# A two-layer prefix DiT block on one core: the opening of layer 0 rearranged by quarters of scale and shift

## The chip, the cores and the metric

The kernel runs on one core of a Trainium2 chip. A core has TensorE (PE, with its weight loads shown as PEld), VectorE (DVE), ScalarE (ACT), GpSimd (POOL) and SyncE (SP), which here only issues transfers. The metric is the device time of one execution in microseconds: the median of three runs is 1883.46 us, from 1881.46 to 1883.66.

## The reference, cut to what matters

256 tokens of 2048 features and 256 context tokens go through two layers. The change touches layer 0, the Fourier branch, for both streams:

```python
shift, scale, gate = split(silu(c) @ ada_w[i] + ada_b[i], 3)
h = _rmsnorm(x, norm_g[i]) * (1 + scale) + shift
def _fourier_branch(h, w_in, w_mix):          # D_BRANCH = 4096
    u, z = split(h @ w_in, 2)                 # u: 16 groups of 256
    f = fft2(ug, axes=(1, 3), norm='ortho').real
    f = einsum('bngc,gcd->bngd', f, w_mix)
    return f * silu(z)
x = x + gate * (y @ w_out[i])
```

The context stream does the same with its own scale, shift and gate from c_ctx. Layer 1 is windowed attention with a sink, and a final norm follows; neither is touched.

## The kernel before, in words

All products are made of three passes: each fp32 operand is split into a high part h, rounded to a faster matrix type on ACT, and a rest l, on DVE (split, L60 and L61), and mm3 (L73 to L75) adds wh·xh, wh·xl and wl·xh in PSUM. The features of the model lie on the partitions in 16 blocks k of 128; both streams stand side by side in 512 columns. The layer has five stages.

- The opening (L148 to L322). The tokens xn come in four tiles of 128 rows, their squares are summed on ACT (L162) and the root taken (L81 to L85). In each of four steps of 512 features, the tokens are scaled by r and split (xh, xl: L212, L213), and a DFT over the tokens is made on PE, 12 passes per k, into PSUM. PE also works on the scale and the shift: `ada_pe` (L180) multiplies 32 pieces of ada_w of 1 MB, in_awp, by the conditioning; `ada_fin` turns a row of 512 results to the partitions (L184, L187, L188). `evac_hx` (L193 to L198) scales the transformed tokens with 1 + scale as it takes them out of PSUM into hx. The shift touches only column 0 of the transform (f0, L310 to L314). While the 16 pieces of shift come in, parts of groups 0 and 1 and the special columns run in between (u_step, sp_step), placed by a list of positions.
- The middle stage (from L329): 16 groups, each with a part "m" and a part "p" of 48 passes, weights wu loaded as sums and differences (load_uh, L122 on POOL and L123 on DVE), a small combined matrix (load_m) and a `mix` of 14 passes that writes two of 32 blocks of 128 features to DRAM (fd).
- The gate stage: 32 blocks z, 48 passes of 512 columns each. Its input hs is made anew from x transposed in DRAM (xT), with r, scale and shift (make_hs, L446 to L448). The first four blocks accumulate side by side over k; the other 28 come one by one. z_out (L455, L456) applies silu and multiplies the block that came back from fd. From block 4 on, each block also takes one job of the row sums for the other scales (ada_jobs, L418, on DVE).
- The output product of layer 0 (32 steps), with the rest of those jobs.
- Layer 1.

The order on each engine is chosen by a scheduler from the written order and its own estimate of times; `issue_after` adds an order by hand. Large weights pass through `raw`, three buffers of 1 MB, on SP's queue; in the opening raw_st adds two more (raw2), so that five are in turn. `ws` has six buffers of half splits, `act` 34 tiles of 128x512, PSUM eight banks. hx fills 32 of the 34 act tiles.

Of the kernel before, what the change touches and what calls it, by code (L numbers as in the profile page):

```python
# [10 lines left out]
F32 = mybir.dt.float32  # L11
# [12 lines left out]
GD = 256  # L24
EPS = 1e-6
# [3 lines left out]
def tile_dit(ctx: ExitStack, tc: tile.TileContext, a: dict, out: bass.AP):  # L29
# [113 lines left out]
    hx = []  # L143
    us = ctx.enter_context(ExitStack())
    sta = ctx.enter_context(ExitStack())
    sx = sta.enter_context(tc.tile_pool(name="sx", reuse_waits="tile", bufs=1))
    with tc.tile_pool(name="st", reuse_waits="tile", bufs=1, side="right") as st:
        xn = [sx.tile([P, D], F32, name=f"xn{t}") for t in range(4)]  # L148
        pre = {}
        pre[1, 0, 0] = raw(a["awp"][1, 0, 0])  # L150
        for t in range(4):
            nc.sync.dma_start(xn[t], a["x2"][t * P : (t + 1) * P, :])
        dump = st.tile([P, D], F32, tag="raw2", name="dump", bufs=2)
        dm = sx.tile([P, 2, N], F32, name="dm")
# [4 lines left out]
        ss = st.tile([P, 4], F32, name="ss")  # L159
        rr = st.tile([P, 4], F32, name="rr")  # L160
        for t in range(4):
            S.activation(dump, xn[t], AF.Square, accum_out=ss[:, t : t + 1])  # L162
            r1 = rsqrt(st, ss[:, t : t + 1], 1, f"r{t}")
            V.tensor_copy(rr[:, t : t + 1], r1)
# [3 lines left out]
        def raw_st(src):  # L168
            cnt[0] += 1
            if cnt[0] % 5 < 3:  # L170
                return raw(src)
            t = st.tile([P, D], F32, tag="raw2", name="raw2", bufs=2)
            nc.sync.dma_start(t[:, : src.shape[-1]], src)
            return t

        def ada_pe(o, which, nb, kgs):
            for kg in kgs:
                t = pre.pop((which, nb, kg)) if (which, nb, kg) in pre else raw_st(a["awp"][which, nb, kg])
                for j in range(4):
                    PE.matmul(o[j * 32 : (j + 1) * 32, :], c32[:, kg * 4 + j, :], t[:, j * 512 : (j + 1) * 512], start=kg == 0, stop=kg == 3)  # L180

        def ada_fin(o, dst, add):
            rows = st.tile([P, 512], F32, tag="rows", name="rows")
            S.copy(rows, o)  # L184
            o2 = psum()
            for j in range(4):
                PE.matmul(o2[:, j * 2 : (j + 1) * 2], rows[:, j * P : (j + 1) * P], sel, start=True, stop=True)  # L187
            V.tensor_tensor(dst, o2[:, 0:8].rearrange("p (a b) -> p a b", b=2), add, op=ALU.add)  # L188

        def evac_hx(nb, os_):  # L190
            for j in range(4):
                o, k = os_[j], nb * 4 + j
                V.tensor_tensor(f0[:, k, :], o[:, 0::N], gs0[:, k, :], op=ALU.mult)  # L193
                h, l = act(F32R), act(F32R)
                for s in range(2):
                    q = slice(s * N, (s + 1) * N)
                    S.activation(h[:, q], o[:, q], AF.Copy, scale=gs0[:, k, s : s + 1])
                    V.scalar_tensor_tensor(l[:, q], o[:, q], gs0[:, k, s : s + 1], h[:, q].bitcast(F32), op0=ALU.mult, op1=ALU.subtract)  # L198
                hx.append((h.rearrange("p (s j) -> p s j", s=2), l.rearrange("p (s j) -> p s j", s=2)))

        f0 = st.tile([P, KT, 2], F32, name="f0")
        prev = None
        for nb in range(4):
            oa = psum()
            ada_pe(oa, 1, nb, (0, 1))
            if prev is not None:
                evac_hx(nb - 1, prev)
            xh = sx.tile([P, 4, 512], F32R, tag="xh", name="xh")
            xl = sx.tile([P, 4, 512], F32R, tag="xl", name="xl")
            for t in range(4):  # L210
                xs = xn[t][:, nb * 512 : (nb + 1) * 512]
                V.tensor_scalar(xh[:, t], xs, rr[:, t : t + 1], None, op0=ALU.mult)  # L212
                V.scalar_tensor_tensor(xl[:, t], xs, rr[:, t : t + 1], xh[:, t].bitcast(F32), op0=ALU.mult, op1=ALU.subtract)  # L213
            prev = []
            for j in range(4):
                o = psum()
                for s in range(2):
                    for tt in range(2):
                        q = slice(j * P, (j + 1) * P)
                        mm3(o[:, s * N : (s + 1) * N], xh[:, s * 2 + tt, q], xl[:, s * 2 + tt, q], dh[:, tt, :], dl[:, tt, :], tt == 0, tt == 1)  # L220
                prev.append(o)
            ada_pe(oa, 1, nb, (2, 3))
            kq = slice(nb * 4, nb * 4 + 4)
            g4 = gs0[:, kq, :]
            ada_fin(oa, g4, adab[:, 0, 1, kq])
            V.scalar_tensor_tensor(g4, g4, 1.0, ng[:, 0, kq], op0=ALU.add, op1=ALU.mult)
# [53 lines left out]
        for nb in range(4):  # L280
            oa = psum()
            for kg in range(4):
# [6 lines left out]
                if pos == 2:  # L289
                    evac_hx(3, prev)  # L290
# [792 lines left out]
```

## Time and profile before

| what | value |
|---|---|
| median of 3 runs | 1883.46 us |
| span of the profiled execution | 1885.9 us (2.4 us above that median; no other time of it is given) |
| PE busy | 97% of the span |
| DVE, ACT, POOL busy | 75%, 50%, 13% |
| bytes moved by DMA | 359.61 MB, mean 191 GB/s |
| first 140 us | 47.63 MB, mean 340 GB/s |
| largest transfers of the opening | 32 pieces in_awp of 1 MB, 4 tiles of tokens, weights wu |

The page gives busy shares per engine and, in 40 slices of 47 us, the busy tenths, the granted TensorE clock and the DMA share. Matmuls are pipelined, so a busy PE isn't PE at its peak: the count of passes in a stretch tells its pace. A table by stretches shows busy time and count for each engine, then clock, DMA share and GB/s. A row of instructions has: line, engine, operation, output and inputs, count, busy time, mean in ns, and the idle time before it with what ended it.

### The profile page before, as it was taken

The page shows a single profiled execution, that of the slowest core. Times are in us where ns is not written, and L with a number is a line of the kernel's source. Part 1 is how long each engine was busy: PE and PEld are TensorE (multiplying, and loading weights), DVE is VectorE, ACT ScalarE, POOL GpSimd, SP SyncE. Part 2 cuts the span into 40 slices and gives each one's busy share as a digit, 9 for nine tenths or more (in the row PEclk, how much of TensorE's full clock was granted, in tenths as well). Part 3 has the DMA queues.
Part 4 walks back from the last instruction along what each step waited for, and adds up shares of the span by engine and source line. Part 5 has one row for each costly group of instructions (what it writes and reads, how often), then busy time and mean ns, then how long its engine had stood idle before and what let it go on. Part 6 is the DMA issues. An engine that isn't in the chain of part 4 may idle for free.

```text
span 1885.9 us, 26510 instructions
## 1 busy us (share of the span) xinstructions
PE 1832.5 (97%) x9921; PEld 1557.9 (83%) x9921; DVE 1412.7 (75%) x2743; ACT 941.1 (50%) x1634; POOL 239.3 (13%) x206
## 2 busy tenths in 40 slices
PE   6889999999999999999999999999999999999997
PEld 4569999888888888888888787888888888887886
DVE  5558999788777779687984744788788878887455
ACT  3334444442222233323322524788888888896443
POOL 0024344200000000000000001102211220200001
PEclk9899999999999999999999999999999999999999
DMA  9975555646656546764576323433333333434553
GB/s 384 381 258 181 196 195 180 233 173 253 243 207 255 213 190 228 285 223 158 199 263 264 112 96 128 138 131 124 123 134 124 123 120 130 176 134 162 196 179 134
DMA packets 60529, 359.61 MB, mean 191 GB/s; under 512 B 7601, under 2 KB 7745, under 8 KB 25329
## 3 DMA queue, kind: packets, MB, share of 16 engines
q1 hardware_dynamic: 49104, 324.83, 47.5%
q0 software_dynamic: 6720, 25.34, 3.6%
q10 hardware_dynamic: 4576, 7.74, 1.2%
q8 instruction: 78, 1.28, 0.3%
q14 instruction: 51, 0.41, 0.1%
HBM read 345.30 MB, written 12.59 MB: 190 GB/s over the span
## 4 chain that ended last, share of the span: by engine, by line
PE 88%; DVE 4%; DMA 3%; issue 3%; ACT 2%; POOL 1%; ACTq 0%; POOLq 0%; DVEq 0%; SPq 0%
PE ps L73 22%; PE ps L74 22%; PE ps L75 22%; PE ps L782 6%; PE ps L784 3%; PE ps L838 3%; PE ps L180 2%; PE ps L853 2%; PE ps L852 2%; PE ps L818 1%; PE ps L819 1%; DMA raw<-in_awp 1%; DVE wpl L61 1%; DMA raw<-in_wu 1%; POOL wm L122 0%
## 5 line engine op out<-in xcount | busy, mean ns | idle before, releaser
L60 ACT CAST wh<-raw 128x1024 fp32r<-128x1024 f32 x333 | 349.7, 1052 | 560.0 <-PE ps L74 485.7
L61 DVE TENSOR_TENSOR wl<-raw,wh 128x1024 fp32r<-128x1024 f32 x333 | 421.4, 1268 | 258.7 <-ACT wh L60 256.3
L74 PE MATMUL ps<-act,wh 128*128 128x512 f32 x1024 | 399.1, 390 | 0.0
L73 PE MATMUL ps<-act,wh 128*128 128x512 f32 x1024 | 394.9, 390 | 0.0
L75 PE MATMUL ps<-act,wl 128*128 128x512 f32 x1024 | 391.9, 390 | 0.0
L73 PEld LDWEIGHTS ps<-act,wh 128*128 128x128 f32 x1024 | 192.9, 188 | 40.1
L75 PEld LDWEIGHTS ps<-act,wl 128*128 128x128 f32 x1024 | 192.8, 188 | 40.1
L74 PEld LDWEIGHTS ps<-act,wh 128*128 128x128 f32 x1024 | 192.8, 188 | 40.0
L782 PE MATMUL ps<-h,wh 128*128 128x512 f32 x512 | 187.0, 400 | 0.0
L418 DVE CUSTOM_DVE_ANT_0 raw<-raw,cb 128x512 f32<-128x512 f32 x256 | 172.6, 688 | 16.3 <-DMA raw<-in_adw 12.5
L418 DVE CUSTOM_DVE_ANT_0 junk<-raw,cb 128x512 f32<-128x512 f32 x192 | 131.6, 686 | 12.1 <-ACT cb L410 6.9
L784 PE MATMUL ps<-h,wl 128*128 128x256 f32 x512 | 138.1, 280 | 0.0
L74 PE MATMUL ps<-wl,h 128*128 128x512 f32 x320 | 126.0, 394 | 1.5 <-DVE wl L61 1.5
L73 PE MATMUL ps<-wh,h 128*128 128x512 f32 x320 | 124.8, 398 | 0.2 <-ACT h L601 0.2
L75 PE MATMUL ps<-wh,h 128*128 128x512 f32 x320 | 124.1, 391 | 0.0
L782 PEld LDWEIGHTS ps<-h,wh 128*128 128x128 f32 x512 | 96.2, 188 | 19.0
L122 POOL TENSOR_TENSOR wm<-raw 128x1016 f32<-128x1016 f32 x32 | 85.7, 2678 | 181.6 <-DMA raw<-in_wu 180.5
L820 DVE CUSTOM_DVE_ANT_0 ps<-ps,mask,nsink 128x512 f32<-128x512 f32 x128 | 92.1, 753 | 12.2 <-PE ps L819 11.3
L823 ACT ACTIVATE p<-ps,mx 128x512 f32<-128x512 f32 x128 | 87.3, 687 | 24.8 <-DVE mx L820 24.2
L784 PEld LDWEIGHTS ps<-h,wl 128*128 128x128 f32 x512 | 96.8, 189 | 1.4
L61 DVE TENSOR_TENSOR pl<-ps,ph 128x512 fp32r<-128x512 f32 x128 | 83.7, 684 | 10.0 <-ACT ph L60 8.8
L828 ACT ACTIVATE p<-p,sm 128x512 f32<-128x512 f32 x128 | 85.4, 716 | 7.8 <-DVE sm L826 7.8
(302 smaller groups left out, 3649.8 us busy)
## 6 DMA issues: line engine op xcount, KB each, us to landing
raw<-in_wz SPq DMA_DIRECT2D x64, 1024.0 KB, 4.9
raw<-in_adw SPq DMA_DIRECT2D x64, 1024.0 KB, 4.9
raw<-in_awp SPq DMA_DIRECT2D x32, 1024.0 KB, 9.1
raw<-in_wo SPq DMA_DIRECT2D x32, 1024.0 KB, 5.6
raw<-in_wq SPq DMA_DIRECT2D x32, 1024.0 KB, 4.8
raw<-in_wu SPq DMA_DIRECT2D x32, 1016.0 KB, 5.2
raw<-in_wo1b SPq DMA_DIRECT2D x16, 1024.0 KB, 4.8
act<-in_xT POOLq DMA_DIRECT2D x32, 256.0 KB, 5.3
```

Source lines behind the costliest of these rows:

```text
L60: S.copy(h, src)
L61: V.tensor_tensor(l, src, h.bitcast(F32), op=ALU.subtract)
L73: PE.matmul(o, wh, xh, start=start, stop=False)
L74: PE.matmul(o, wh, xl, start=False, stop=False)
L75: PE.matmul(o, wl, xh, start=False, stop=stop)
L122: GP.tensor_tensor(m, v[:, :, 0, :], v[:, :, 1, :], op=ALU.subtract)
L418: V.tensor_tensor_reduce(junk if s == 0 and i < 3 else wf, wf, cb[:, s, kq * 512 : kq * 512 + 512], 1.0, 0.0, ALU.mult, ALU.add, acc[:, i, ...
L782: PE.matmul(o[0], wh[:, q], hx1[k], start=k == 0, stop=k == KT - 1)
L784: PE.matmul(o[0][:, 0:N], wl[:, q], hx1[k][:, 0:N], start=False, stop=False)
L820: V.tensor_tensor_reduce(o, o, mask[:, tb, :], -0.125, nsink[:, i : i + 1], ALU.add, ALU.min, mx[:, tb : tb + 1])
L823: S.activation(pt[:, tb, :], so[tb], AF.Exp, bias=mx[:, tb : tb + 1], scale=-1.0, accum_out=sm[:, tb : tb + 1])
L828: S.activation(pt[:, tb, :], pt[:, tb, :], AF.Copy, scale=sm[:, tb : tb + 1])
```

## The change

The opening is written anew. NE = 6 gate blocks of layer 0 are computed inside it.

- Tokens are loaded as 16 tiles of 512 features; squares are taken per tile, per stream (`norm`). Each token tile is also turned on PE (`turn_x`), 64 turns, copied from PSUM by DVE.
- The DFT runs first, unscaled, and is copied to `rawx` by ACT; `hx_prep` later multiplies by the scale and puts the shift into column 0.
- Scale and shift come in the order of quarters: for each i the four pieces of scale, then the four of shift, then their turns. As soon as a quarter of both is there, z_x makes the gate input of its four k from the turned tokens, and z_step adds 18 passes per k into six PSUM banks. z_load and z_w bring 1.5 MB of gate weights per quarter and split them. At the end silu is applied and the six gates go to DRAM (zd).
- Groups 0 and 1 and the special columns are no longer interleaved: all groups run alike after the opening. Only the weights of group 0 are loaded and split in the last quarter. The constants cst and wsp, and load_m(0), come after the opening.
- The gate stage starts with blocks 6 to 9 side by side (weights read as four runs of 512 columns per row), multiplies blocks 0 to 5 by the gates read back from zd, and has 22 single blocks. The 28 jobs are spread over these 22 (two on every fourth), and each job sums 1024 columns at a time instead of 512.

```diff
+NE = 6
-        for t in range(4):
-            nc.sync.dma_start(xn[t], a["x2"][t * P : (t + 1) * P, :])
+        for t in range(4):
+            xn.append([act() for _ in range(4)])
+            for c in range(4):
+                nc.sync.dma_start(xn[t][c], a["x2"][t * P : (t + 1) * P, c * 512 : (c + 1) * 512])
+        def norm(s):
+            for t in (2 * s, 2 * s + 1):
+                for c in range(4):
+                    dump = wsp.tile([P, 512], F32, tag="ws", name="dump")
+                    S.activation(dump, xn[t][c], AF.Square, accum_out=ss[:, t, c : c + 1])
...
+        def dft(s, c):
+            for tt in range(2):
+                S.activation(xh[:, tt], xn[t][c], AF.Copy, scale=rr[:, t : t + 1])
+                V.scalar_tensor_tensor(xl[:, tt], xn[t][c], rr[:, t : t + 1], xh[:, tt].bitcast(F32), ...)
+            for kp in (2 * c, 2 * c + 1):
...
+                rawx[kp][s] = act()
+                S.copy(rawx[kp][s], o)
+        def turn_x(s, c):
+            for kp in (2 * c, 2 * c + 1):
...
+                        PE.transpose(o[:, ...], xn[2 * s + tt][c][:, q], ident)
+                V.tensor_copy(xT[kp][s], o)
+        def z_load(i):
+            wa = raw_st(a["wz0"][i])
+            wb = raw_st(a["wz"][0 : NE - 4, :, i * 512 : (i + 1) * 512].rearrange("b p c -> p b c"), NE - 4)
+        def z_w(i, wa, wb):
+            pa = [half_split(wa, j) for j in range(2)]
+            for b in range(NE - 4):
+                h, l = ext(F32R), ext(F32R)
+                split(h, l, wb[:, b * 512 : (b + 1) * 512])
+        def z_x(k):
+            for s in range(2):
+                V.scalar_tensor_tensor(t, t, gs0[:, k, s : s + 1], r_bc[:, q], op0=ALU.mult, op1=ALU.mult)
+                S.activation(h[:, q], t, AF.Identity, bias=sh0[:, k, s : s + 1])
+                V.scalar_tensor_tensor(l[:, q], t, sh0[:, k, s : s + 1], h[:, q].bitcast(F32), op0=ALU.add, op1=ALU.subtract)
+        def z_step(k, bs=range(NE)):
+            for b in bs:
+                mm3(zo[b], *zw[k][b], *zx[k], k == 0, k == KT - 1)
+        for c in range(4):
+            turn_x(0, c)
+        norm(0)
+        dft(0, 0)
+        dft(0, 1)
+        ada(0, 1, 0)
+        dft(0, 2)
+        norm(1)
+        ada(0, 1, 1)
+        dft(0, 3)
+        for c in range(4):
+            turn_x(1, c)
+        bcast_rows(rr, r_bc)
+        ada(0, 1, 2)
+        dft(1, 0)
+        ada(0, 1, 3)
+        rows = rows_of(1)
+        dft(1, 1)
+        turn(0, 1, rows)
+        wr = z_load(0)
+        ada(0, 0, 0)
+        dft(1, 2)
+        ada(0, 0, 1)
+        dft(1, 3)
...
+        z_w(0, *wr)
+        ada(0, 0, 2)
+        ada(0, 0, 3)
+        turn(0, 0, rows_of(0))
+        for i in range(4):
+            k = 4 * i
+            for j in range(4):
+                z_x(k + j)
+                if j == 0:
+                    hx_prep(k)
+            if i < 3:
+                ada(i + 1, 1, 0)
+                ada(i + 1, 1, 1)
+            z_step(k)
+            hx_prep(k + 1)
+            if i < 3:
+                ada(i + 1, 1, 2)
+                ada(i + 1, 1, 3)
+                rows = rows_of(1)
+            z_step(k + 1)
+            if i < 3:
+                turn(i + 1, 1, rows)
+                wr = z_load(i + 1)
+                ada(i + 1, 0, 0)
+                ada(i + 1, 0, 1)
+            else:
+                wur = [load_uh(0, kh, raw_st) for kh in range(2)]
+            hx_prep(k + 2)
+            z_step(k + 2)
+            if i < 3:
+                z_w(i + 1, *wr)
+                ada(i + 1, 0, 2)
+                ada(i + 1, 0, 3)
+                rows = rows_of(0)
+            else:
+                wu0.extend(split_uh(*w) for w in wur)
+            hx_prep(k + 3)
+            z_step(k + 3, early)
+            if i < 3:
+                turn(i + 1, 0, rows)
+            z_step(k + 3, late)
+        for b in range(NE):
+            z = ext()
+            S.activation(z, zo[b], AF.Silu)
+            nc.gpsimd.dma_start(zd[b], z)
...
-            for kq in range(2):
-                wf = w[:, f * 1024 + kq * 512 : f * 1024 + kq * 512 + 512]
+            wf = w[:, f * 1024 : (f + 1) * 1024]
...
-                if b >= 4:
-                    with tc.issue_after(hs_end[0]) if b < 8 else nullcontext():
-                        next(ada)
+                if b >= NE + 4:
+                    with tc.issue_after(hs_end[0]) if b < NE + 8 else nullcontext():
+                        for _ in range(2 if b % 4 == 2 else 1):
+                            next(ada)
...
-            for b in range(4):
+            for b in range(NE + 4):
                 with tc.issue_after(last_dma[0]):
                     nc.sync.dma_start(ys[b], fd[b])
             for b in range(4):
-                z_out(b, o4[b])
-            for b in range(4, NB):
+                z_out(NE + b, o4[b])
+            for b in range(NE):
+                z = zp.tile([P, 512], F32, tag="z", name="z")
+                with tc.issue_after(last_dma[0]):
+                    nc.sync.dma_start(z, zd[b])
+                V.tensor_tensor(ys[b], ys[b], z, op=ALU.mult)
+            for b in range(NE + 4, NB):
```

More of the change, by code (lines that the diff above doesn't have):

```diff
@@ L143, in tile_dit @@
     hx = []
+    rawx = [[None, None] for _ in range(8)]
     us = ctx.enter_context(ExitStack())
@@ L166, in tile_dit, with raw_st @@
         cnt = [0]
-        def raw_st(src):
+        def raw_st(src, nb=0):
             cnt[0] += 1
             if cnt[0] % 5 < 3:
-                return raw(src)
-            t = st.tile([P, D], F32, tag="raw2", name="raw2", bufs=2)
-            nc.sync.dma_start(t[:, : src.shape[-1]], src)
-            return t
[L176 to L180, printed above, removed]
@@ L185, in ada_fin, with turn @@
+        def turn(i, which, rows):
             o2 = psum()
@@ L201, in tile_dit @@
[L201 to L226, printed above, removed]
```

270 lines of the change are left out of this document (145 added, 125 removed).

## The prediction

> **What bounds the kernel now.** I read the page first, then the opening in stretches of ten microseconds, then PE's waits, then PE in order of time.
>
> ```profile
> span 1885.9 us, 26510 instructions
> PE 1832.5 (97%) x9921; PEld 1557.9 (83%) x9921; DVE 1412.7 (75%) x2743; ACT 941.1 (50%) x1634; POOL 239.3 (13%) x206
> PE   6889999999999999999999999999999999999997
> PEclk9899999999999999999999999999999999999999
> DMA  9975555646656546764576323433333333434553
> ```
>
> PE is the bound nearly everywhere, and only the first three slices (47 us each) are short of nine tenths; there DMA has its only nines. So a gain must come out of the first 140 us.
>
> ```profile
> 0.00:10.00 10.00, 1.93 (x8) 0.23 (x8) 0.35 (x2) 1.51 (x2) 1.23 (x9) 1.00 0.79 290
> 10.00:20.00 10.00, 5.45 (x24) 5.28 (x24) 5.75 (x22) 8.52 (x9) 1.66 (x3) 1.00 1.02 425
> 50.00:60.00 10.00, 9.25 (x69) 5.41 (x68) 7.22 (x20) 3.40 (x9) 0.00 (x0) 1.00 0.80 316
> 80.00:90.00 10.00, 9.24 (x48) 5.97 (x45) 3.56 (x15) 2.06 (x4) 0.00 (x0) 0.59 1.02 418
> 130.00:135.00 5.00, 0.81 (x3) 0.50 (x2) 4.97 (x6) 2.66 (x6) 3.52 (x3) 0.76 0.63 217
> 0.00:120.00 120.00, 95.65 (x667) 61.88 (x668) 58.38 (x165) 38.14 (x65) 12.85 (x17) 0.93 0.95 373
> 180.00:200.00 20.00, 20.00 (x169) 20.00 (x169) 18.64 (x25) 9.54 (x18) 7.53 (x5) 1.00 0.55 198
> 359.00:707.00 348.00, 348.00 (x1536) 288.20 (x1536) 267.64 (x615) 106.71 (x139) 3.19 (x6) 1.00 0.58 215
> ```
>
> The columns are PE, PEld, DVE, ACT and POOL busy with their counts, the granted clock, the DMA share and GB/s. The loads run at a share of 0.95 for 120 us, and PE waits for them or runs at 0.59 of its clock; at 130 to 135 DVE is full and PE empty. The last two rows give PE's full-rate prices: 20/169 = 0.118 us for a pass of 256 or 260 columns (the middle stage), 348/1536 = 0.227 us for one of 512 columns (the 32 gate blocks of 48).
>
> ```profile
> PE ps L180 <- DMA raw<-in_awp: 14.2, 4, 7.0
> PE ps L73 <- DVE xh L212: 5.6, 1, 5.6
> PE ps L187 <- ACT rows L184: 5.2, 7, 0.8
> PE ps L379 <- DVE asp L360: 3.1, 1, 3.1
> PE ps L74 <- DVE ml L61: 2.7, 1, 2.7
> 14.55 0.55 PE L73 MATMUL ps<-dh,xh 128*128 128x256 f32 x1 [5.58 <-DVE xh L212]
> 16.40 1.05 PE L75 MATMUL ps<-dh,xl 128*128 128x256 f32 x4
> 121.00 1.92 PE L180 MATMUL ps<-raw,c 128*32 128x512 f32 x16
> 123.68 1.05 PE L187 MATMUL ps<-sel,rows 128*128 128x2 f32 x8 [0.76 <-ACT rows L184]
> 139.14 0.42 PE L73 MATMUL ps<-act,wph 128*127 128x260 f32 x1
> 1056.27 2.78 PE L546 MATMUL ps<-ident,act 128*128 128x128 f32 x24
> ```
>
> The first rows are PE's waits of the opening (total, times, longest). At 139.14 the second part of group 1 starts; from there both kernels do the same middle stage. That is my mark.
>
> **How much of 139.1 us is loss.** Full-rate work on PE before the mark: 32 pieces of scale and shift at 0.96 (half the L180 row) = 30.7; 8 turns at 1.05 = 8.4; the token transform, 2 streams x 16 k x 2 token tiles x 3 = 192 passes at 0.118 = 22.7; three parts of groups 0 and 1 and the special columns, 4 x 48 = 192 passes = 22.7; two load_m of 10 passes and one mix of 14 = 4.0; the broadcast of r, 8 short passes, about 1. Sum 89.5. The loss is 139.1 - 89.5 = 49.6 us. It is all the change can win.
>
> **The change, part by part.**
>
> Six gate blocks move under the opening: 6 x 48 = 288 passes, 65.3 us at 0.227, and the same 65.3 leave the gate stage, where PE has no gap. The 192 passes of groups 0 and 1, with load_m and mix, move out behind the opening. On PE these moves cancel; only losses count.
>
> Added: 64 turns of tokens. The L546 row has 24 such turns in 2.78, so 0.116 each, 7.4 us in all.
>
> The Trainium skill, "TensorE: Matmul & The Clock Gate", Part 4, speaks against this part: it says a turn on PE takes about 275 ns in a kernel and does not release the clock gate. By its figure 64 turns are 17.6 us, an estimate from that page, and the sum ends 10 us later. The row with 0.116 us, right behind dense passes, disagrees.
>
> Work of the new opening on PE: 30.7 + 8.4 + 22.7 + 1 + 65.3 + 7.4 = 135.5 us, if it never waited. Can the other engines keep up?
>
> ```profile
> L162 ACT ACTIVATE dump<-xn 128x2048 f32<-128x2048 f32 x4 | 7.6, 1910 | 8.0 <-DMA xn<-in_x 8.0
> L184 ACT COPY rows<-ps 128x512 f32<-128x512 f32 x8 | 4.7, 586 | 48.6 <-PE ps L180 48.6
> L197 ACT ACTIVATE act<-ps,gs 128x256 fp32r<-128x256 f32 x32 | 12.6, 485 | 9.0 <-DVE f L193 7.1 <-DVE act L198 1.9
> L198 DVE SCALAR_TENSOR_TENSOR act<-ps,gs,act 128x256 fp32r<-128x256 f32 x32 | 13.2, 475 | 1.4 <-ACT act L197 1.4
> L213 DVE SCALAR_TENSOR_TENSOR xl<-xn,rr,xh 128x512 fp32r<-128x512 f32 x16 | 11.2, 746 | 0.1
> L61 DVE TENSOR_TENSOR wl<-raw,wh 128x1024 fp32r<-128x1024 f32 x5 | 6.1, 1222 | 1.3 <-ACT wh L60 1.3
> L60 ACT CAST wh<-raw 128x1024 fp32r<-128x1024 f32 x5 | 5.2, 1045 | 2.7 <-DMA raw<-in_wz 2.7
> L61 DVE TENSOR_TENSOR pql<-ps,pqh 128x512 fp32r<-128x512 f32 x14 | 9.5, 678 | 0.0
> L313 DVE CAST act<-f 128x2 fp32r<-128x2 f32 x16 | 1.5, 163 | 0.1
> 1.66 2.52 SPq L152 DMA_DIRECT2D xn<-in_x  x4
> L478 SPq DMA_DIRECT2D y<-fd x4: 326/356/382, 352.1 to 366.9; - x4
> ```
>
> One quarter (four k) costs PE 72 passes of 0.227, 8 pieces and 2 turns: 16.3 + 7.7 + 2.1 = 26.1 us. DVE has in it 16 two-operand passes of z_x and 8 of hx_prep, 24 x 0.475 = 11.4, weight splits 2 x 1.22 + 2 x 0.68 = 3.8, and some 20 small ones of 0.16 = 3.2: 18.4 us. ACT has 16 halves at 0.485, splits 2 x 1.05 + 2 x 0.59, two copies of rows: 12.2 us. Both fit under PE; if DVE lagged by its whole excess in the last quarter (18.4 plus the splits of group 0, four at 1.22 and two sums, 25.7 against PE's bare 16.3), it would cost up to 9 us behind it.
>
> Loads: 32 pieces, tokens, four gate quarters of 1.5 MB come before the last shift, 42 MiB = 44.0 MB, some 0.5 more of constants. The opening of before moved 373 GB/s x 120 us = 44.8 MB by 120 us, so the same pace ends at about 119 us. Behind that stand the last piece and a bare quarter, 18 us: 137 us is what loads force. PE forces 135.5 plus its losses. The five 1 MB buffers turn over as before, but two of every ten now wait for splits on ACT and DVE instead of for PE.
>
> SP issues the tokens in 16 pieces of 256 KB instead of 4 of 1 MB: at 0.356 (the L478 row, same size) 5.7 us for 2.5, still less than the ten that tokens take to land, and the first pieces of scale stand only behind them. POOL gets six gate writes and no new wait; its queue has room at 13%.
>
> Losses on PE, by the written order (a scheduler places the instructions, so places are approximate). Start: the first transform still waits for tokens, squares (1.9 us per 2048 columns, cut in four and a little dearer), the root and a split. Tokens come first now; I keep 14.5 us for the first pass (row 14.55), with half the turns (3.7) done before it: 10.8 lost. Between 0 (turns fill it) and 14.5 in the range. Cold clock after it: four passes in 1.05, 0.26 against 0.118; five and a half microseconds at half rate, 2.7. ACT in the transform has 8 x 4 x 0.586 = 18.8 plus squares of the second stream, 6, under 37 us of PE work: nothing, unless its order blocks. Before the first gate step a chain DVE, ACT, DVE of 0.475 + 0.485 + 0.475 twice over hangs on the shift: 2. At three quarter borders the same chain is half covered by the nine "late" passes (2.0): 1 each, 3 in all; between 0 and 9.1 us each, the time an exposed load would take (row in the rivals). Sum 18.5, so the gate blocks end near 154 us.
>
> Behind it: constants, special columns and load_m(0) now start there, beside groups 0 and 1. Before paid 3.1 + 2.7 of waits and a cold clock at that place. Their loads stand in ACT's queue and may have to wait for memory of the gate tiles, with ACT's splits behind them. I take 4; the bounds are 0 and 9 (the DVE lag above).
>
> Gate stage: ten blocks are read back instead of four at its start and six finished gates come by DMA, 4 MB in a 43 us stretch at a DMA share of 0.58: nothing. If they blocked SP's queue, the three weight buffers still cover a block of 10.9 us. The 28 row jobs of layer scales now sit on 22 blocks, two on every fourth, with sums over 1024.
>
> ```profile
> L418 DVE CUSTOM_DVE_ANT_0 raw<-raw,cb 128x512 f32<-128x512 f32 x256 | 172.6, 688 | 16.3 <-DMA raw<-in_adw 12.5
> 707.00:755.00 48.00, 48.00 (x214) 39.74 (x213) 45.05 (x100) 16.30 (x22) 0.00 (x0) 1.00 0.62 230
> raw<-in_awp SPq DMA_DIRECT2D x32, 1024.0 KB, 9.1
> ```
>
> A sum of 512 takes 0.688. From 256 to 512 columns a DVE pass grows from 0.475 to 0.746 (L198, L213), so 512 more cost 0.54 and a sum of 1024 near 1.23, less than two of 512: DVE gains a little per job. PE kept 214 passes in 48 us with DVE at 45.05, two jobs a step: nothing for PE either way.
>
> Sum: 49.6 - 7.4 - 18.5 - 4 = 19.7 us gained. The profiled span of 1885.9 stands 2.4 above the median of 1883.46 (0.13%); no other time of that execution is given. I take the difference off the median: 1864.
>
> **The rivals.** (a) Exposed loads, slower. A quarter holds two of five buffers until ACT and DVE have split them, SP issues in order, and PE stands before the next piece. One landing (9.1 us, last row) exposed in each of four quarters costs 36: 1900. It decides from 19.7/4 = 4.9 us per quarter, or a mean load pace under 44.5/155 = 287 GB/s. For it: 14.2 us of such waits now, with a worst full stretch of 316. Against: a quarter needs 9.96 MB in 26.1 us, 382 GB/s, and stretches at 418 and 425 stand above.
>
> (b) Loads set the pace mildly: at 316 GB/s the last shift lands at 141, the gates end at 159, five later: 1869, and with the stage change at its bound of 9, 1874.
>
> (c) Turns stay at half clock because little surrounds them at the start: the cold rows double a pass, 64 x 0.23 = 14.8 instead of 7.4: 1871. This is the way of the Trainium skill's rule in the same part of that page; the granted clock over the turns would show it.
>
> (d) The gate passes fill everything: 11 us lost in all and no stage change cost: 1852.
>
> (e) The gap goes nowhere: gates hide, but groups 0 and 1 stall on DVE by all of its lag (5 more) and the four quarters by 3.7 each: 1884.
>
> **How the numbers follow.** Forecast 0.47, its own range 1855 to 1876; (a) 0.19; (b) 0.15; (c) 0.08; (d) 0.06; (e) 0.05. This kernel's three runs span 0.12%, so 0.2% (3.8 us) is about what can be told. Faster: 0.47 + 0.15 + 0.08 + 0.06 = 0.76; same 0.05; slower 0.19. From 1852 to 1887 leaves out most of (a) above and half of (d) below, under 2 in 10.
>
> **What would show it.** Gates ending between 146 and 165 us, PE at nine tenths or more from 55 us on, clock 1.00 there; the first transform pass near 14.5; turns near 0.12; group 1's second part about 27 us (226 passes) plus under 9 behind the last gate pass; 26 gate blocks left at 10.9 each. It is wrong if PE's waits for in_awp or for the z_x tiles pass 5 us in a quarter, or if the stage change or the gate stage opens new gaps.

## The result, and the profile after

The changed kernel takes 1880.13 us in the median (1875.82 to 1889.48), the kernel before 1883.46 beside it (1880.37 to 1889.39), 15 runs each. The ratio is 0.9984, with an interval from 0.9971 to 0.9997: faster by 3.3 us, 0.16%, where 19.7 us were forecast and the prediction put what can be told at 0.2%. The profiled executions stand further apart, 1885.9 us of span before and 1877.6 after, 8.3 us. The page of the changed kernel:

```profile
span 1877.6 us, 26414 instructions
PE 1837.9 (98%) x9985; PEld 1562.2 (83%) x9985; DVE 1419.6 (76%) x2363; ACT 976.6 (52%) x1726; POOL 246.8 (13%) x210
PE   7999999999999999999999999999999999999997
PEclk9999999999999999999999999999999999999999
DMA  8894555565776756664585323333333333434543
```

PE has 7 tenths in the first slice instead of 6 and nine in the next two, where it had eight: the gaps of the opening are gone, as was meant. The stretches say the same (columns as before: PE, PEld, DVE, ACT and POOL busy with counts, clock, DMA share, GB/s):

```profile
0.00:10.00 10.00, 3.92 (x14) 2.47 (x15) 1.42 (x4) 5.34 (x14) 1.23 (x9) 1.00 0.78 259
10.00:20.00 10.00, 4.48 (x22) 4.08 (x21) 6.32 (x19) 8.57 (x25) 1.42 (x2) 0.88 0.98 363
50.00:60.00 10.00, 10.00 (x83) 7.47 (x85) 4.82 (x12) 4.31 (x8) 0.00 (x0) 1.00 0.58 204
80.00:90.00 10.00, 10.00 (x58) 6.47 (x58) 0.59 (x2) 0.59 (x1) 0.00 (x0) 1.00 1.00 382
140.00:150.00 10.00, 8.04 (x40) 5.18 (x41) 4.61 (x19) 4.25 (x9) 4.70 (x2) 0.87 0.45 172
200.00:400.00 200.00, 196.72 (x1615) 194.80 (x1613) 194.95 (x235) 92.45 (x179) 88.05 (x54) 1.00 0.58 198
```

From 50 to 140 us PE is busy for 88.5 of 90 us at a clock of 1.00. What is left stands at the start, at 140 to 150, and, in the last row, in the middle stage: there DVE is busy for 195 of 200 us and PE for 197. PE's waits in the whole run:

```profile
PE ps L218 <- DMA act<-in_x: 6.1, 3, 4.7
PE ps L74 <- ACT xh L199: 5.5, 1, 5.5
PE ps L74 <- ACT mh L61: 3.4, 1, 3.4
PE ps L239 <- ACT rows L233: 2.2, 3, 0.8
PE ps L76 <- DVE wml L62: 2.0, 4, 0.8
PE ps L75 <- DVE apl L62: 1.3, 3, 0.8
PE ps L74 <- ACT ext L276: 1.2, 1, 1.2
```

The wait for in_awp, 14.2 us before, has gone altogether. The first two are the start. The fourth and the last are the chains at quarter borders; mh, wml and apl are splits that PE waits for in the middle stage. PE in order of time, at the places that the next sections speak of:

```profile
19.59 0.58 PE L74 MATMUL ps<-dh,xh 128*128 128x256 f32 x1 [5.52 <-ACT xh L199]
37.75 1.91 PE L218 MATMUL ps<-ident,act 128*128 128x128 f32 x16
39.59 1.05 PE L229 MATMUL ps<-raw,c 128*32 128x512 f32 x2
41.15 1.06 PE L229 MATMUL ps<-raw,c 128*32 128x512 f32 x6
55.08 1.06 PE L229 MATMUL ps<-raw,c 128*32 128x512 f32 x8
56.08 0.38 PE L74 MATMUL ps<-dh,xh 128*128 128x256 f32 x1
56.30 0.28 PE L75 MATMUL ps<-dl,xh 128*128 128x256 f32 x1
142.36 1.92 PE L229 MATMUL ps<-raw,c 128*32 128x512 f32 x16
145.04 1.05 PE L239 MATMUL ps<-sel,rows 128*128 128x2 f32 x8 [0.76 <-ACT rows L233]
147.30 2.08 PE L74 MATMUL ps<-ext,wh 128*128 128x512 f32 x4 [1.20 <-ACT ext L276]
165.71 0.40 PE L76 MATMUL ps<-ext 128*128 128x512 f32 x1
412.18 0.63 PE L74 MATMUL ps<-act,wh 128*128 128x512 f32 x1
```

The gates end at 166.1 us (forecast 154), the gate stage starts at 412.18. So the profile splits into three parts:

| part | before | after | what the moves alone would give | difference |
|---|---|---|---|---|
| opening, to the mark or to the end of the gates | 139.1 | 166.1 | 154 by the forecast | 12.1 worse |
| from there to the gate stage | 217.1 (356.21 - 139.14) | 246.1 | 217.1 + 226 passes, 26.7, = 243.8 | 2.3 lost, 4 forecast |
| the rest of the span | 1529.7 | 1465.4 | 1529.7 - 65.3 = 1464.4 | 1.0 worse |

19.7 - 12.1 + 1.7 - 1.0 = 8.3, the measured difference of the two spans. So in this pair the shortfall against the forecast, 11.4 us, is the opening's: the middle stage cost less than the 4 us set aside for it. The other 5 us to the medians are the spread of single executions, which is 9 us or more for both kernels. A run's time stands 1.7 to 2.1 us above its span (1879.40 for 1877.6 in the profiled run of the changed kernel), so the profiled execution of the kernel before took about 1887.8 us by estimate, 4.3 above its median, and that of the changed kernel 0.7 below its own.

### The profile page after: what moved, and what is told of

Read it like the earlier page. It is cut to its first block, busy times and chain, and to the rows that moved or that the text cites. A ratio compares the mean times of both kernels' runs of the same rounds, so it can differ in the third digit from the quotient of the medians.

```text
span 1877.6 us, 26414 instructions
## 1 busy us (share of the span) xinstructions
PE 1837.9 (98%) x9985; PEld 1562.2 (83%) x9985; DVE 1419.6 (76%) x2363; ACT 976.6 (52%) x1726; POOL 246.8 (13%) x210
## 5 line engine op out<-in xcount | busy, mean ns | idle before, releaser
L61 ACT CAST wh<-raw 128x1024 fp32r<-128x1024 f32 x329 | 345.1, 1051 | 464.7 <-PE ps L75 361.0
L62 DVE TENSOR_TENSOR wl<-raw,wh 128x1024 fp32r<-128x1024 f32 x329 | 416.4, 1269 | 213.1 <-ACT wh L61 210.3
L75 PE MATMUL ps<-act,wh 128*128 128x512 f32 x928 | 362.0, 390 | 0.0
L74 PE MATMUL ps<-act,wh 128*128 128x512 f32 x928 | 358.9, 390 | 0.0
L76 PE MATMUL ps<-act,wl 128*128 128x512 f32 x928 | 356.9, 390 | 0.0
L74 PEld LDWEIGHTS ps<-act,wh 128*128 128x128 f32 x928 | 174.8, 188 | 36.4
L76 PEld LDWEIGHTS ps<-act,wl 128*128 128x128 f32 x928 | 174.7, 188 | 36.4
L75 PEld LDWEIGHTS ps<-act,wh 128*128 128x128 f32 x928 | 174.8, 188 | 36.2
L513 DVE CUSTOM_DVE_ANT_0 raw<-raw,cb 128x1024 f32<-128x1024 f32 x128 | 155.1, 1222 | 24.4 <-DMA raw<-in_adw 23.2
L513 DVE CUSTOM_DVE_ANT_0 junk<-raw,cb 128x1024 f32<-128x1024 f32 x96 | 117.2, 1221 | 26.4 <-DMA raw<-in_adw 16.5
L123 POOL TENSOR_TENSOR wm<-raw 128x1016 f32<-128x1016 f32 x32 | 90.6, 2833 | 214.3 <-PE ps L75 121.6
```

The lines of the kernel that those rows point to most:

```text
L61: S.copy(h, src)
L62: V.tensor_tensor(l, src, h.bitcast(F32), op=ALU.subtract)
L74: PE.matmul(o, wh, xh, start=start, stop=False)
L75: PE.matmul(o, wh, xl, start=False, stop=False)
L76: PE.matmul(o, wl, xh, start=False, stop=stop)
L123: GP.tensor_tensor(m, v[:, :, 0, :], v[:, :, 1, :], op=ALU.subtract)
```

## The experiments

"First pass" is PE's first pass of the transform, "gates end" the end of its last gate pass in the opening (in the kernel before, the start of group 1's second part), "stage" the time from there to the gate stage's first pass. All from the profiled execution of each kernel; the medians are of all its runs. Where a recorded text has a gates' end 0.4 us earlier or a stage 0.4 us longer, it counts from the start of the last gate pass. In "difference on DVE" and "idle POOL" 28 passes of group 0 ran ahead of the last gate pass, in all the others with gates 2 to 4: those 24 passes make the gates end 2.8 us later and the stage 2.8 us shorter there.

| run | first pass | gates end | stage | span | median | ratio to before, interval |
|---|---|---|---|---|---|---|
| kernel before | 14.55 | 139.1 | 217.1 | 1885.9 | 1883.46 | |
| before, again | 14.42 | 140.7 | 215.9 | 1883.9 | one run, 1885.74 | |
| before, difference on DVE | 14.26 | 139.6 | 210.2 | 1877.5 | 1881.54 | 0.9991 [0.9979, 1.0002] |
| changed kernel | 19.59 | 166.1 | 246.1 | 1877.6 | 1880.13 | 0.9984 [0.9971, 0.9997] |
| changed, again | 19.99 | 166.3 | 250.3 | 1880.8 | 1883.79 | 1.0006 [0.9992, 1.0019] |
| root first | 16.93 | 166.8 | 247.7 | 1878.7 | 1886.24 | 1.0020 [0.9996, 1.0044] |
| late half behind the turn | 21.08 | 171.3 | 247.6 | 1885.2 | 1887.45 | 1.0027 [1.0012, 1.0041] |
| four gates | 19.71 | 148.7 | 249.1 | 1884.7 | 1884.20 | 0.9996 [0.9980, 1.0012] |
| third buffer | 21.20 | 166.0 | 247.0 | 1877.9 | 1880.50 | 0.9978 [0.9958, 0.9997] |
| tokens by DMA | 25.80 | 169.0 | 251.7 | 1886.8 | 1884.99 | 0.9999 [0.9980, 1.0018] |
| whole pieces | 17.95 | 161.6 | 257.3 | 1882.7 | 1879.94 | 0.9977 [0.9960, 0.9993] |
| difference on DVE | 19.44 | 168.5 | 235.3 | 1867.0 | 1868.91 | 0.9921 [0.9908, 0.9933] |
| all together | 19.06 | 163.4 | 235.9 | 1862.4 | 1863.15 | 0.9887 [0.9873, 0.9900] |
| idle POOL | 21.60 | 170.4 | 263.7 | 1896.5 | 1898.57 | 1.0074 [1.0054, 1.0094] |

**Both kernels again**, with no edit.

> The changed kernel, a second time, to see how much of a stage's length is its own. If its opening is paced by its own order, the first transform pass stands again near 19 to 20 us and the gates end again at 166, within 1; if transfers pace it, these move with the run by several us. Time 1880, 1876 to 1889 as before.

> The kernel before, profiled a second time. Its own time on fifteen runs spans 1880.4 to 1889.4, and the profile on which the prediction rests had a span of 1885.9. If that profile was an ordinary run, group 1's second part begins again at 139 us, within 1; if it was a late one, it begins 2 to 5 us earlier, and the 49.6 us of loss counted there were too many by as much.

The changed kernel's median is now 1883.79 and the ratio's interval holds 1: the gain is between nothing and 0.3%, not more. Its opening came out the same within 0.4 us, but its stage took 250.3 instead of 246.1. The kernel before differs in its two profiles by 1.6 in the opening and 1.2 in the stage; its opening came out later and not earlier, so the count of 49.6 us did not rest on a late profile. The sum for this second pair of profiles: 19.7 forecast, 12.3 worse in the opening, 1.6 better because the kernel before was later there, 250.3 - 215.9 - 26.7 = 7.7 in the stage instead of 4, and 2.2 worse in the rest (1464.2 for 1527.3 - 65.3): 3.1, again the difference of the spans.

**Root first.** In the start, DVE does its work in a fixed order, and the profile of the changed kernel shows what stood before the root of the first stream:

```profile
12.16 0.15 DVE L191 TENSOR_REDUCE s<-ss 128x2 f32<-128x8 f32 x1
12.23 2.58 DVE L220 COPY act<-ps 128x512 f32<-128x512 f32 x4
14.72 0.16 DVE L82 TENSOR_SCALAR r0v<-s 128x2 f32<-128x2 f32 x1
18.13 0.16 DVE L191 TENSOR_REDUCE s<-ss 128x2 f32<-128x8 f32 x1 [2.18 <-ACT dump L189]
18.20 0.15 DVE L85 SCALAR_TENSOR_TENSOR r0s<-r0s,r0v 128x2 f32<-128x2 f32 x1
18.59 0.20 DVE L192 COPY rr<-r0r 128x2 f32<-128x2 f32 x1
```

Four copies of turned tokens stand between the sum (12.16) and its first use (14.72), and the sum of the *second* stream (18.13, 2.18 us of waiting for ACT) ahead of the last steps of the first one's root. The edit orders both behind it:

```diff
+        norm(0)
         for c in range(4):
             turn_x(0, c)
-        norm(0)
...
+            with tc.issue_after(root[0]) if s else nullcontext():
                 V.tensor_reduce(s2[:, q], ss[:, q, :], axis=AX.X, op=ALU.add)
+                with tc.issue_after(root[0]) if s == 0 and kp > 2 else nullcontext():
                     V.tensor_copy(xT[kp][s], o)
```

> Only the order on DVE at the start is changed: the root of the first stream's squares is finished before the copies of turned tokens and before the sum of the second stream. Theory A (PE and its chains pace the opening, the start is lost to DVE's order): the first transform pass comes at 14 to 15.5 instead of 19.4 us and the gates end 3 to 5 us earlier, time 3 to 5 us less. Theory B (loads pace the opening): the first pass comes earlier too, but the gates end within 1 us of before, time the same.

The first pass came 2.7 us earlier (16.93, not the 14 to 15.5 of theory A), the gates ended 0.7 later. PE waited for nothing new; it had more visits to the pieces of scale and shift. A piece is four products of 512 columns whose results go to four groups of 32 rows. In PE's rows above, one such product alone (x2 records, at 39.59) holds PE for 1.05 us, the other three (41.15) for 1.06, and all four together (55.08) for 1.06. The Trainium skill, "TensorE: Matmul & The Clock Gate", Part 3, says that small products into different column groups run side by side in the array; these rows agree. A scheduler that puts transform passes between the four pays twice. Up to 43 us root first took seven visits for four pieces, the changed kernel five, and up to the first gate pass its visits sum to 15.95 us, those of the changed kernel to 13.70: 2.25 of the 3.4 us that were lost again. "Whole pieces" below tests that.

**Late half behind the turn.** At the last border PE has nothing to cover the chain from the last pieces to the first gate pass (rows from 142.36 to 147.30). The edit keeps nine passes of each quarter's last k for it, behind the last product of the turn:

```diff
-                turn(i + 1, 0, rows)
-            z_step(k + 3, late)
+                last = turn(i + 1, 0, rows)
+            with tc.issue_after(last) if i < 3 else nullcontext():
+                z_step(k + 3, late)
```

> Only one order on PE is added: the last nine passes of each quarter's gate step stand behind the turn of the next quarter's shift, as written. In the changed kernel all of the third quarter's passes ran ahead of the last two pieces of shift, and the chain from those pieces to the last quarter lay bare from 142.4 to 147.3 us, with a cold clock behind it. Theory A: nine passes cover about 2.1 us of that chain, and the clock stays up: gates end 2 to 4 us earlier. Theory B (the last pieces of shift land late): PE waits for them instead, named in the waits, and the gates end where they did.

The gates end 5.2 us later, 1.5 of them from the start, and the time is longer. The edit holds the passes at all three borders, where two had them in a good place: PE's waits for rows went from 2.2 to 2.9 us, and a new one of 3.2 us for the low part of z_x (ext) appeared.

**Four gates.** `NE = 4`, and no second weight tile per quarter (the 28 jobs are spread over 24 blocks):

```diff
-NE = 6
+NE = 4
-            wb = raw_st(a["wz"][0 : NE - 4, :, i * 512 : (i + 1) * 512].rearrange("b p c -> p b c"), NE - 4)
+            wb = None
```

> Four gate blocks in the opening instead of six; two more stand in the gate stage (96 passes, 21.8 us), and 2 MB less is loaded in the opening. Theory A (PE paces the opening): it gets 96 passes shorter, 20 to 23 us, gates end at 143 to 146, and the time is the same within 4 us. Theory B (loads and their buffers pace it): the opening shrinks only by the 2 MB, about 5 us, and the time grows by 13 to 17 us.

The gates end 17.5 us earlier, at 148.7, less than theory A had it and far more than theory B; the two blocks cost 1486.9 - 1465.4 = 21.5 in the gate stage. So the last two of the six hide 4 us in the opening and pay the rest in full: with six, PE is nearly the bound there.

**Third buffer.** The last pieces of shift were issued at 120 to 131 us, each waiting for a free tile. With three raw2 tiles (and 13 `ext` tiles instead of 16):

```diff
-            if cnt[0] % 5 < 3:
+            if cnt[0] % 6 < 3:
-                t = st.tile([P, D], F32, tag="raw2", name="raw2", bufs=2)
+                t = st.tile([P, D], F32, tag="raw2", name="raw2", bufs=3)
```

> A third extra 1 MB buffer for the loads of the opening (six in turn instead of five; room is made by 13 small gate tiles instead of 16). Theory A (PE and chains pace the opening): the gates end within 2 us of 166. Theory B (loads wait for buffers, and the last shift lands late for that): the last pieces land 4 to 8 us earlier and the gates end 4 to 6 us earlier, time 4 to 6 us less.

The gates end where they did (166.0), though the first pass was 1.6 later, so no more than about that can be the buffer's. Buffers don't set the pace of the opening; that the loads ended near 140 us and not at 119 cost little, because PE was full.

**Tokens by DMA.** No turns on PE; POOL's queue brings the turned tokens from DRAM:

```diff
-                        PE.transpose(o[:, kk * N + tt * P : kk * N + (tt + 1) * P], xn[2 * s + tt][c][:, q], ident)
-                xT[kp][s] = act()
-                V.tensor_copy(xT[kp][s], o)
...
+                xk.append(act())
+                nc.gpsimd.dma_start(xk[-1], a["xT"][:, len(xk) - 1, :])
```

> The turned tokens come from DRAM, where they lie turned, by 16 transfers of 256 KB on POOL's queue; the 64 turns on PE and their copies on DVE are gone. Theory A (PE paces the opening): 64 turns of 0.116 go, and DVE's copies no longer delay the first root: gates end 7 to 10 us earlier. Theory B (loads pace it): 4.2 MB more, 10 to 12 us at 373 GB/s, make the gates end up to 10 us later.

64 turns fewer on PE, and the gates end 2.8 us later: the first pass moved to 25.80, since beside the extra transfers the tokens came in so that ACT took the last square at 23 us. From the first pass to the gates' end it took 143.2 us instead of 146.5. The turns of the first stream fill a gap that is there anyway, so their going won nothing.

**Whole pieces.** Root first, and an order by hand that keeps a piece's four products together up to the first gate block (`behind()` orders them after PE's last transform pass, and the next passes and turns after them):

```diff
+        def behind():
+            return tc.issue_after(pe_at[0]) if pe_at[0] else nullcontext()
...
+            with behind():
+                for j in range(4):
+                    last = PE.matmul(oa[which][j * 32 : (j + 1) * 32, :], c32[:, kg * 4 + j, :], ...).ins
+            if i == 0:
+                pe_at[0] = last
```

> The root of the first stream goes first, as in the run with the root first, and besides the four products of a piece of scale or shift are kept together on PE up to the first gate block (a piece is four products of 512 columns into four groups of 32 rows; in the rows one product alone takes 1.05 us and four together 1.06). Theory A, the visits set the price: the run with the root first won 2.7 us at the first pass (16.93 for 19.59) and lost it again because its pieces were torn into 7 visits where 4 would do; whole, the first transform pass stays near 17 and the gates end at 166.4 - 4 x 0.97 = 162.5. Theory B, loads or the chains of the later quarters set the end: the gates end between 165.5 and 166.5, as in all kernels with six gate blocks and the old order at the end. Time by A: 3 to 4 us under the changed kernel, by B the same.

Theory A held for the opening: the visits ahead of the first gate pass sum to 11.10 us, 4.9 less than in root first; the first gate pass comes at 61.4 instead of 65.8, and the gates end at 161.6, 5.2 earlier than in root first, 4.5 earlier than in the changed kernel. Yet the profiled span is 5.1 *longer* than the changed kernel's: the stage behind the gates took 257.3. PE's waits there:

```profile
PE ps L76 <- DVE wml L62: 8.2, 11, 1.2
PE ps L74 <- ACT mh L61: 3.9, 1, 3.9
PE ps L74 <- ACT wmh L61: 2.9, 3, 1.6
```

In this profile what the opening won was given back in the middle stage. It was one of the kernel's slower executions, 1884.46 us: the runs go from 1871.05 to 1885.67, a wider spread than that of any other kernel but root first, with the median at 1879.94.

**Difference on DVE.** Why would the same sixteen groups take 246 us once and 257 another time? The groups of DVE work from 200 to 400 us in the changed kernel (instructions, count, busy us, mean ns, idle before), with POOL's:

```profile
L123 POOL TENSOR_TENSOR wm<-raw 128x1016 f32<-128x1016 f32 x25 | 72.4, 2896 | 80.6 <-DMA raw<-in_wu 80.6
L62 DVE TENSOR_TENSOR wpl<-raw,wph 128x1016 fp32r<-128x1016 f32 x28 | 53.5, 1912 | 0.0
L62 DVE TENSOR_TENSOR wml<-wm,wmh 128x1016 fp32r<-128x1016 f32 x27 | 32.8, 1214 | 1.0
L62 DVE TENSOR_TENSOR ml<-mt,mh 128x512 fp32r<-128x512 f32 x13 | 25.6, 1971 | 0.0
```

Two splits of the same size, 1912 and 1214 ns on average; and the split of m takes 1971 ns, where the prediction's row of the same size from PSUM (pql) has 678. DVE in order of time, in the changed kernel:

```profile
247.15 1.21 DVE L62 TENSOR_TENSOR wpl<-raw,wph 128x1016 fp32r<-128x1016 f32 x1
248.27 0.43 DVE L62 TENSOR_TENSOR apl<-ps,aph 127x260 fp32r<-127x260 f32 x1
248.61 2.55 DVE L62 TENSOR_TENSOR ml<-mt,mh 128x512 fp32r<-128x512 f32 x1
254.56 3.40 DVE L62 TENSOR_TENSOR wpl<-raw,wph 128x1016 fp32r<-128x1016 f32 x1
```

and POOL in the same stretch:

```profile
247.41 3.19 POOL L123 TENSOR_TENSOR wm<-raw 128x1016 f32<-128x1016 f32 x1 [2.19 <-DMA raw<-in_wu]
254.25 2.64 POOL L123 TENSOR_TENSOR wm<-raw 128x1016 f32<-128x1016 f32 x1 [3.65 <-DMA raw<-in_wu]
```

The split at 254.56 starts 0.3 us after POOL's difference and ends 1.07 after it (257.96 against 256.89): it stood until POOL was done. So did the one at 248.61. The split at 248.27, whose input is in PSUM, ran beside POOL at its usual 0.43. The Trainium skill, "SBUF — State Buffer", section "SBUF: two separate sides", says that DVE and GpSimd share one pair of ports, held by one of them for a whole instruction, and that a DVE operation with two inputs in SBUF needs it; these rows agree. In the 200 us every operation of DVE that took more than 1.5 times its least had both inputs in SBUF. The edit, one engine's name:

```diff
-        GP.tensor_tensor(m, v[:, :, 0, :], v[:, :, 1, :], op=ALU.subtract)
+        V.tensor_tensor(m, v[:, :, 0, :], v[:, :, 1, :], op=ALU.subtract)
```

> The difference of the two halves of a weight block (wm) is taken on DVE instead of POOL. In the changed kernel DVE is busy for 195 of the 200 us from 200 to 400, and PE waits there for its splits. Theory A, POOL and DVE get in each other's way: a split of the sum takes 1.21 us alone and up to 3.43 while POOL works (53.5 us for 28), a split of m 0.675 and up to 2.56 (25.6 for 13). Without POOL that is 19.6 + 16.8 less, and 26 differences at 1.21 = 31.5 more: DVE 190, its splits all at 1.21 and 0.68, the stretch from the last gate pass to the gate stage 241 to 245 where two profiles have 246.1 and 250.7, PE's waits for splits under 4 (7.1 and 10.4), time 2 to 6 us less. Theory B, the slow splits come from something else: they stay, DVE has 226 us of work for 200, and the time is some 25 us longer.

The same stretch, 200 to 400 us, and the same groups:

```profile
200.00:400.00 200.00, 200.00 (x1662) 200.00 (x1661) 186.87 (x264) 95.44 (x180) 17.72 (x33) 1.00 0.61 206
```

```profile
L62 DVE TENSOR_TENSOR wpl<-raw,wph 128x1016 fp32r<-128x1016 f32 x27 | 32.6, 1208 | 1.3 <-ACT wph L61 1.2
L123 DVE TENSOR_TENSOR wm<-raw 128x1016 f32<-128x1016 f32 x26 | 31.4, 1209 | 1.0 <-DMA raw<-in_wu 1.0
L62 DVE TENSOR_TENSOR ml<-mt,mh 128x512 fp32r<-128x512 f32 x14 | 9.6, 684 | 0.1
```

DVE took on 26 differences, 31.4 us, and is busy *less* (187 instead of 195). PE has no gap left in these 200 us. The stage takes 235.3 us, 238.1 with the 24 early passes, 3 us below what was expected; the time is 1868.9, 11 us under the changed kernel where 2 to 6 were expected, with all five runs between 1868.79 and 1872.38.

**The same in the kernel before**, and **all together** in the changed one (root first, whole pieces, third buffer, difference on DVE).

> The same move of the difference to DVE in the kernel before. Its middle stage shows DVE splits of 1.84 and 2.14 us on average too, but PE waits only 4.7 us for them. If the changed kernel loses in its middle stage what it won in the opening because DVE sets the pace there, this kernel gains less than the changed one: 0 to 3 us. If it gains as much, the middle stage doesn't tell the two kernels apart.

> Root first, whole pieces, a third load buffer and the difference on DVE together in the changed kernel. If the opening is limited by visits and start (A above) and the middle stage by DVE: gates end near 162, the stretch behind them 241 to 245, both gains add: 1872 to 1876. If a gain in the opening is given back in the middle stage whatever DVE does: 1877 to 1880, as the third buffer alone.

The kernel before gains 3.4 us in the median, just over what was expected, with an interval that holds 1; its stage falls from 215.9 and 217.1 to 210.2 in the profile, which was the quickest of its runs. So with the blocking gone the change is worth 1881.54 - 1868.91 = 12.6 us, where with it the two kernels stand 3.3 and -0.8 apart. All together takes 1863.15 us, 1.1% under the kernel before and the fastest of all, 9 below what was expected. Against the difference alone its gates end 5.1 us earlier, its stage is 0.6 longer, its span 4.6 shorter; with the 24 early passes counted alike, the opening is 2.3 shorter and the stage 2.2. So a gain in the opening is no longer given back.

**Idle POOL.** The difference moved off POOL also reaches ACT and PE sooner (1.2 us instead of 2.9). To tell that from the blocking, POOL gets its work back, for nobody:

```diff
         V.tensor_tensor(m, v[:, :, 0, :], v[:, :, 1, :], op=ALU.subtract)
+        for q in (slice(0, 4), slice(4, 8)):
+            GP.tensor_tensor(junkd, m[:, q], m[:, q], op=ALU.subtract)
```

> As the run with the difference on DVE, which ended its middle stage 235.7 us after the gates and took 1868.9 us; now POOL subtracts each difference from itself in two halves and nobody reads what it writes. Theory A, the two engines block each other: DVE's splits grow again (1.21 and 0.68 alone, up to 3.4 and 2.55 beside POOL); DVE had 187 us of work in 200, so some 30 us more make it the bound: the stage behind the gates takes 246 to 265 and the time is 1879 to 1898. Theory B, the slow part of the changed kernel was POOL's 2.8 us of delay for the difference, in place of DVE's 1.2: nobody waits for POOL here, so the stage stays at 236 and the time at 1869.

From 200 to 400 us:

```profile
200.00:400.00 200.00, 188.43 (x1515) 183.71 (x1514) 198.89 (x239) 87.21 (x163) 85.31 (x75) 1.00 0.52 180
L125 POOL TENSOR_TENSOR junkd<-wm 128x508 f32<-128x508 f32 x50 | 71.8, 1435 | 83.9 <-DVE wm L123 81.9
L62 DVE TENSOR_TENSOR wpl<-raw,wph 128x1016 fp32r<-128x1016 f32 x25 | 36.5, 1461 | 0.0
```

DVE is full, PE waits, the stage takes 263.7 and the time 1898.57, 30 us over the kernel without that work and 0.6 above the end of theory A's range. The splits beside POOL take up to 2.2 us here (POOL's halves last 1.4 each); those that POOL leaves alone keep their 1.20. It is the blocking.

## Why the prediction was right or wrong

The gain was a sixth of the forecast: 1880.13 us lies above the forecast's own 1855 to 1876, and the sign of so small a gain was lost when both kernels ran again (-0.8). Two steps of the prediction failed. The first, the sum of the opening's losses, failed in every profile with six gate blocks: they end at 161.6 us or later. The second, the middle stage, shows when the blocking is taken away: the change is then worth 12.6 us in the medians, so of the 16.4 us that are missing some 9 go with the blocking and some 7 with the rest, the opening above all. By its steps:

- **"Sum 18.5, so the gate blocks end near 154 us."** This step failed: of 166.1 us, 135.5 are work, so 30.6 were lost, 12.1 more than the sum. Start: 19.59 less 3.7 of turns, 15.9 for 10.8. Cold passes behind it, 0.21 us apart until 24.6: about 2.2 for 2.7. First chain and borders: waits of 2.2 for rows and 1.2 for ext, and 1.7 of half-rate passes from 147.30 on, 5.1 for 5. Not in the sum at all: two torn pieces, 1.9; sixteen pieces that came alone, 1.00 and 0.10 for the change behind them (56.30 - 56.08 is 0.22, not 0.12) instead of 0.96, 2.2; gate passes at 0.233 instead of 0.227 in the opening, 288 x 0.0063 = 1.8; four passes of group 0 that ran ahead, 0.5. That makes 29.6; 1.0 is not assigned.
- **"From there both kernels do the same middle stage."** This step failed too. The work is the same, the time is not: the stage took 216 and 217 us in the kernel before and, less the 26.7 us of passes moved into it, 219 to 231 in the seven profiles with six gates in the opening and the difference on POOL. The prediction had quoted the row, DVE at 18.64 of 20 us from 180 to 200, and read only PE's price from it; for DVE's limit it looked at the opening and at the jobs of the gate stage. With the blocking, DVE is busy for 195 of 200 us (in the kernel before, from 145 to 345 us, for 189, with PE at 198); what PE saves ahead of that can be lost there. Its term for the change of stage, 4 us with bounds 0 and 9, measured 2.3 and 7.7 in the two pairs of profiles, so its size held there, for another reason than the one given (constants and splits at its start), and 257.3 - 217.1 - 26.7 = 13.5 in "whole pieces". Without the blocking it is 235.9 - 210.2 - 26.7 = -1.0 in "all together" and, with the 24 early passes counted, 1.2 in "difference on DVE".
- **The first pass near 14.5.** It came at 19.59, by DVE's order (root first: 16.93). It was costed as the same chain as before; the copies of the turns and the second stream's sum stood in it.
- **Turns at 0.12.** 16 in 1.91 us, right, with the clock up. The first 32 ran at half that pace, 26 in 5.99 us, as rival (c) had it, but in time in which PE waited for tokens and the root; no cost of it shows. That turns do not release the clock, the rule of the Trainium skill, "TensorE: Matmul & The Clock Gate", Part 4, does not hold here (its figure in isolation is for bf16, these turns are fp32). In the changed kernel the trace's first record of the granted clock is 1.00 at 14.2 us, after PE had done nothing but these turns (before it nothing is recorded, and the 1.00 in the row 0:10 says nothing of them). In root first it comes at 11.85 us, while the turns still run: up to there they start every 0.213 us, from there every 0.109.
- **Quarter 26.1 and 1.** Three quarters, from the end of the first quarter's last piece (61.1 us) to that of the last (144.3), took 83.2, 27.7 each for 27.1: right within 0.6. PE at nine tenths from 55 us on: right, but for the 140 to 150 stretch.
- **Loads.** Rivals (a) and (b) are out: no wait for in_awp, and a third buffer moved the gates' end by 0.1. SP needed 10.1 us for the 16 pieces of tokens, not 5.7: 0.63 each, where the row it was taken from has 0.356. The prediction's row of the opening before, 4 pieces of 1 MB in 2.52, has the 0.63.
- **65.3 us leave the gate stage.** Right within 1 to 2 us: the rest fell by 64.3 and 63.1. The sums over 1024 columns took 1.222 us each (1.23 forecast), and two jobs on a block cost nothing.
- **Rival (e), "groups 0 and 1 stall on DVE by all of its lag",** was nearest in time (1884) and named the engine. The rest of it is not what came: the quarters did not stall, and DVE was late not by the last quarter's splits but by its waits for POOL, in all the groups and in both kernels.

What stays open: which executions lose how much in the middle stage. Only profiled ones show it, and they differ by 4 us for one kernel. That the wide spread of these kernels comes from there is suggested by the runs without the blocking, which lie within 3.6 us (4.4 in the kernel before, beside 9.7 with it); but the four runs of idle POOL, with blocking, lie within 2.2, so it is not shown.

## What to carry to other kernels

When another engine is nearly full beside PE in a stage behind the change (here 195 of 200 us), price that stage too: what PE gains ahead of it may be waited away there. Compare the mean time of an instruction with its least before taking a busy share as work: a mean half above it (here 1912 ns for 1202) can be waiting, and the engine that runs beside it is the first suspect. Before comparing two stages, count the instructions in each: a scheduler moves them across the border. A scheduler's small moves have a price of their own, and an order by hand around the few places that matter can give them back.

## What the runs showed of the hardware

- An operation of DVE with both inputs in SBUF that starts while POOL subtracts stands still until POOL is done: 1.21 us became 3.40, 0.68 became 2.55; with an input in PSUM it kept its time (0.43 beside POOL). Moving 31 us of work from POOL *to* DVE made DVE less busy; putting idle work on POOL cost 30 us.
- Four fp32 products of 512 columns that go to four groups of 32 output rows hold PE for 1.06 us, and one of them alone for 1.05.
- Turns of fp32 tokens on PE, alone, brought the granted clock up: in root first they start 0.213 us apart until the first record of 1.00 at 11.85 us and 0.109 apart from there.
- Transfers were issued on SP at 0.63 us apiece at the start, 16 of 256 KB in 10.11 us and, in the kernel before, 4 of 1 MB in 2.52; the 256 KB row of the kernel before has 0.356 at another place.
